# Running sums carried to all partitions by a DRAM scratch and repeating loads, where a selecting matmul did it: a two-layer hybrid block on one NeuronCore

## The chip, the core and the metric

One core of a Trainium2 chip (trn2) runs the whole program in one launch. The metric is the device time of an execution in microseconds (us); lower is better. The kernel before takes 1228.23 us (median of three runs).

## What is computed

The reference passes 256 tokens of width 1024 through two layers. A layer is a gated feed-forward, a mixer and a second feed-forward, each added to the residual. The mixer projects the normed input to 6232 columns: a state-space branch (z, a short convolution, step sizes dt) and an attention branch (q, k, v and an index that picks 64 keys per query). The change touches the state-space branch alone. With one chunk of 256 tokens it comes down to this:

```python
def ssd_chunked(xh, dt, a, bmat, cmat, chunk):
    x = xh * dt[..., None]
    adt = dt * a                                  # 256 tokens x 16 heads
    a_cs = jnp.cumsum(adt, axis=-1)               # the running sums
    seg = a_cs[..., :, None] - a_cs[..., None, :]
    decay = exp(where(tril, seg, -inf))           # 256 x 256 for each head
    cb = einsum('bclgn,bcsgn->bcgls', cc, bc)
    y_diag = einsum('bcgls,bcgels,bcsgep->bclgep', cb, decay, x)
    ...
```

For each of 16 heads the matrix of decays needs the running sum of the column's token (one number a partition, which an engine takes as a per-partition bias) and that of the row's token: a row of 256 numbers that must stand in all 128 partitions. How that row gets to all partitions is what changes.

## The kernel before

All weights stream through three raw buffers of 1 MB (`Stream`): SyncE issues the loads (L113), ScalarE rounds a block to `whi` (L126), VectorE takes the rest as `wlo` (L127), and TensorE multiplies three times, high by high, high by low, low by high (`three`, L181 to L183; the convolution's columns at L887 to L889). Three split blocks exist at a time, so a block is split when TensorE has used up the one three before it.

The mixer (`mixer`) walks `MIX_ORDER`: index columns, z and convolution columns, then q, k and v in units of 512 columns, two token tiles each. A unit's bank is drained by one ScalarE instruction (L915 for q and k, L912 for v), GpSimd rotates q and k (`rope`, L406 to L409), and TensorE transposes them (`turn`, L866). Between these units generators are stepped that hold the side work: `steps` (dt and the running sums), `index` (scores at L655 and L660, then the top 64), `ssd` and `attention`. A scheduler sets the final order of each engine's instructions when the program is built; the engines then run their own lists in order and wait on semaphores.

The steps touched:

- `steps` makes the running sums `cs` (128 tokens x 2 tiles x 16 heads) with three small matmuls. It then splits them into a high and a low part, puts both into `c2` (16 high columns, a gap, 16 low columns), transposes `c2` in two matmuls (L626), and ScalarE copies the result to `csT` (64 x 256, L627).
- `ssd` goes over 2 groups of 8 heads in fours (`h0` of 0 and 4). For each four it takes a tile `m` from `six()` (two buffers, shared with the index's `idx_tm` and `idxT` and later with the attention); `m0` is 4 x 256, `m1` 4 x 128. Per head one matmul (L734) has a column of `pick`, repeated to 128 columns, as its stationary operand and `csT` as its moving one: it adds high and low part of one head's row and puts the row in all partitions of a PSUM bank of pool `sd`. ScalarE reads it twice (L740, L742: Relu of the difference from the per-partition sum), then takes two Exps for the four (L744, L745). VectorE multiplies with `dt` and the masked `cb` (L748, L750).
- After both fours TensorE forms y (L760, L764: 24 matmuls a group into two banks of `ac`); y of the first four can run before the second four is there. GpSimd (L774), VectorE (L780, L781, L788) and ScalarE (L438) finish y, and it is transposed for the output projection (L795).

Of the kernel before, what the change touches and what calls it, by code (L numbers as in the profile page):

```python
# [8 lines left out]
F32 = mybir.dt.float32  # L9
FR = mybir.dt.float32r  # L10
I32 = mybir.dt.int32
AF = mybir.ActivationFunctionType
ALU = mybir.AluOpType
AX = mybir.AxisListType

P = 128
# [36 lines left out]
def hybrid_kernel(  # L53
# [18 lines left out]
    tp = ctx.enter_context(tc.tile_pool(name="tp", bufs=2, space=PSUM))  # L72


    def bank(pool):
        return pool.tile([P, 512], F32, name=pool.name, tag=pool.name)
# [223 lines left out]
    pick_f = const.tile([64, H_SSD], F32, name="pick_f")  # L300
    nc.gpsimd.memset(pick_f, 0.0)
    for base in (0, 32):
        nc.gpsimd.affine_select(out=pick_f, in_=pick_f, compare_op=ALU.not_equal, fill=1.0,
                                base=-base, pattern=[[-1, H_SSD]], channel_multiplier=1)
    pick = const.tile([64, H_SSD], FR, name="pick")
    c2s = []
    for l in range(DEPTH):
        c2 = const.tile([P, NT, 64], F32, name=f"c2_{l}")
        nc.gpsimd.memset(c2, 0.0)
        c2s.append(c2)  # L310
# [24 lines left out]
    def setup():  # L335
# [4 lines left out]
        with tc.tile_pool(name="setup", bufs=1, reuse_waits="tile") as tmp:  # L340
# [15 lines left out]
            nc.vector.tensor_copy(pick, pick_f)  # L356
# [194 lines left out]
    def mixer(l, norm, after):  # L551
        with ExitStack() as mctx:
# [23 lines left out]
            csT = ms.tile([64, L], FR, name="csT")  # L576
# [6 lines left out]
            def steps():  # L583
# [34 lines left out]
                chi = ms.tile([P, NT, H_SSD], FR, name="chi")  # L618
                nc.vector.tensor_copy(chi, cs)
                c2 = c2s[l]  # L620
                nc.vector.tensor_copy(c2[:, :, 0:16], chi.bitcast(F32))
                nc.vector.tensor_sub(c2[:, :, 32:48], cs, chi.bitcast(F32))
                yield
                ps = bank(tp)
                for t in range(NT):
                    nc.tensor.transpose(ps[0:64, t * P:(t + 1) * P], c2[:, t], ident)  # L626
                nc.scalar.copy(csT, ps[0:64, :L])  # L627
# [85 lines left out]
            def ssd():  # L713
# [9 lines left out]
                for g in range(G_SSD):  # L723
                    ms4 = []
                    for h0 in (0, 4):
# [4 lines left out]
                        for h in (0, 2):  # L730
                            ps = bank(sd)
                            for j in range(2):
                                hh = 8 * g + h0 + h + j
                                nc.tensor.matmul(ps[:, j * L:(j + 1) * L],  # L734
                                                 pick[:, hh:hh + 1].to_broadcast([64, P]), csT,
                                                 start=True, stop=True)
# [270 lines left out]
```

## Time and profile before

| | |
|---|---|
| median of three runs | 1228.23 us (1227.38 to 1228.77) |
| the profiled execution's own time | 1228.15 us |
| its span in the trace | 1226.4 us |
| granted TensorE clock, mean | 0.998 |
| TensorE busy | 99% of the span |
| VectorE, ScalarE, GpSimd busy | 60%, 51%, 8% |

The span runs from the first to the last instruction; 1.75 us of the execution lie around it. Layer 0's mixer has its running sums and decays between 255 and 355 us, layer 1's 603 us later.

### The profile page before, as it was taken

The numbers are of one execution on the slowest core, as the hardware profiler recorded it, in microseconds if no ns is written. First come the engines' busy times: TensorE is split into PE (matmuls) and PEld (weight loads), VectorE is DVE, ScalarE is ACT, GpSimd is POOL, SyncE is SP. The second block draws the span as 40 slices with busy tenths as digits, with TensorE's granted clock in tenths as the row PEclk, the third lists the DMA queues.
The fourth block names the chain that finished last, engine by engine and source line by source line (L and its number), as shares of the span: only waits on it lengthen the run. The fifth ranks groups of instructions, "written<-read, shape, count | busy, mean of one in ns | idle before, by whom it ended". The sixth has DMA issues, their size and how long they took to land.

```text
span 1226.4 us, 15386 instructions
## 1 busy us (share of the span) xinstructions
PE 1211.1 (99%) x6031; PEld 1010.0 (82%) x6031; DVE 734.3 (60%) x970; ACT 629.8 (51%) x860; POOL 102.5 (8%) x209
## 2 busy tenths in 40 slices
PE   8999999999999999999999999999999999999997
PEld 6788889988888888888888888898977888888886
DVE  5655545785687565554465554476858866555543
ACT  5544435656676454444354444366567655444432
POOL 0200000601220000000000000024112100000000
PEclk9999999999999999999999999999999999999999
DMA  8665555654233555655646645465442445556550
GB/s 256 195 206 174 187 177 167 213 170 167 99 138 110 166 184 167 199 197 181 201 151 196 197 168 201 158 214 175 155 154 84 157 155 161 179 175 206 179 198 35
DMA packets 147820, 210.02 MB, mean 171 GB/s; under 512 B 7908, under 2 KB 115108, under 8 KB 147748
## 3 DMA queue, kind: packets, MB, share of 16 engines
q1 hardware_dynamic: 147604, 208.52, 51.5%
q8 instruction: 47, 0.77, 0.3%
q10 hardware_dynamic: 144, 0.52, 0.1%
q14 instruction: 25, 0.20, 0.0%
HBM read 207.98 MB, written 1.05 MB: 170 GB/s over the span
## 4 chain that ended last, share of the span: by engine, by line
PE 93%; DVE 3%; DMA 1%; ACT 1%; POOL 1%; issue 0%; SPq 0%; POOLq 0%; ACTq 0%; DVEq 0%
PE mm L181 15%; PE mm L182 15%; PE mm L183 15%; PE ac L183 12%; PE ac L181 12%; PE ac L182 12%; PE tp L522 2%; PE ac L760 1%; PE mm L887 1%; PE mm L889 1%; PE ac L889 1%; PE mm L888 1%; PE ac L887 1%; PE ac L888 1%; DVE wlo L127 1%; PE sd L655 1%
## 5 line engine op out<-in xcount | busy, mean ns | idle before, releaser
L127 DVE TENSOR_TENSOR wlo<-raw,whi 128x2048 fp32r<-128x2048 f32 (+3 forms) x206 | 451.2, 2195 | 337.3 <-ACT whi L126 336.9
L126 ACT CAST whi<-raw 128x2048 fp32r<-128x2048 f32 (+3 forms) x206 | 377.0, 1836 | 304.4 <-PE ac L183 187.1
L181 PE MATMUL mm<-whi,tT 128*128 128x512 f32 (+1 forms) x672 | 268.4, 399 | 0.0
L182 PE MATMUL mm<-wlo,tT 128*128 128x512 f32 (+1 forms) x672 | 260.8, 388 | 2.8 <-DVE wlo L127 2.8
L183 PE MATMUL mm<-whi,tT 128*128 128x512 f32 (+1 forms) x672 | 261.7, 389 | 0.4 <-DVE tT L418 0.4
L181 PE MATMUL ac<-whi,tT 128*128 128x512 f32 (+1 forms) x480 | 190.4, 397 | 0.9 <-ACT whi L126 0.5
L182 PE MATMUL ac<-wlo,tT 128*128 128x512 f32 (+1 forms) x480 | 184.8, 385 | 0.8 <-DVE wlo L127 0.8
L183 PE MATMUL ac<-whi,tT 128*128 128x512 f32 (+1 forms) x480 | 185.4, 386 | 0.0
L182 PEld LDWEIGHTS mm<-wlo,tT 128*128 128x128 f32 x672 | 126.5, 188 | 27.1 <-DVE wlo L127 3.5
L183 PEld LDWEIGHTS mm<-whi,tT 128*128 128x128 f32 x672 | 126.2, 188 | 27.2 <-issue 1.3
L181 PEld LDWEIGHTS mm<-whi,tT 128*128 128x128 f32 x672 | 126.4, 188 | 23.4 <-ACT s L912 0.7
L182 PEld LDWEIGHTS ac<-wlo,tT 128*128 128x128 f32 x480 | 90.4, 188 | 17.7 <-DVE wlo L127 1.8
L181 PEld LDWEIGHTS ac<-whi,tT 128*128 128x128 f32 x480 | 90.2, 188 | 17.8 <-ACT whi L126 1.2
L183 PEld LDWEIGHTS ac<-whi,tT 128*128 128x128 f32 x480 | 90.2, 188 | 17.7
L432 POOL TENSOR_TENSOR r_x<-ms_x,mhalf 128x1 f32<-128x1 f32 x14 | 9.7, 695 | 873.6 <-DVE ms_x L430 866.1
L181 PE MATMUL ac<-whi,hT_hi 128*128 128x512 f32 x176 | 69.3, 394 | 0.0
L181 PE MATMUL mm<-whi,hT_hi 128*128 128x512 f32 x176 | 69.0, 392 | 0.0
L183 PE MATMUL ac<-whi,hT_lo 128*128 128x512 f32 x176 | 68.6, 390 | 0.0
L183 PE MATMUL mm<-whi,hT_lo 128*128 128x512 f32 x176 | 68.6, 390 | 0.0
L182 PE MATMUL mm<-wlo,hT_hi 128*128 128x512 f32 x176 | 68.5, 389 | 0.0
L182 PE MATMUL ac<-wlo,hT_hi 128*128 128x512 f32 x176 | 68.5, 389 | 0.0
L544 ACT ACTIVATE s1k<-ac,r_x 128x256 f32<-128x256 f32 x44 | 20.6, 471 | 67.6 <-PE ac L183 64.7
(222 smaller groups left out, 1463.7 us busy)
## 6 DMA issues: line engine op xcount, KB each, us to landing
raw<-in_w_ffn_in_dram SPq DMA_DIRECT2D x172, 512.0 KB, 4.9
raw<-in_w_ffn_out_dram SPq DMA_DIRECT2D x44, 1024.0 KB, 4.8
raw<-in_w_mix_in_dram SPq DMA_DIRECT2D x44, 1024.0 KB, 5.2
raw<-in_w_mix_out_dram SPq DMA_DIRECT2D x16, 1024.0 KB, 4.8
raw<-in_w_mix_in_dram SPq DMA_DIRECT2D x4, 600.0 KB, 3.8
raw<-in_w_mix_in_dram SPq DMA_DIRECT2D x4, 568.0 KB, 3.8
raw<-in_w_ffn_in_dram SPq DMA_DIRECT2D x8, 256.0 KB, 3.5
h_res<-in_x_dram SPq DMA_DIRECT2D x4, 256.0 KB, 3.6
```

The costliest lines, as they stand in the source:

```text
L126: pin(nc.scalar.copy(hi[:, o], raw[:, o]))
L127: pin(nc.vector.tensor_sub(lo[:, o], raw[:, o], hi[:, o].bitcast(F32)))
L181: nc.tensor.matmul(ps, xh, whi, start=first, stop=False)
L182: nc.tensor.matmul(ps, xh, wlo, start=False, stop=False)
L183: nc.tensor.matmul(ps, xl, whi, start=False, stop=last)
L522: nc.tensor.transpose(ps[:, f * L + t * P:f * L + (t + 1) * P], hs[:, t, f * P:(f + 1) * P], ident)
L544: nc.scalar.activation(sg, ps[:, 0:256], AF.Silu, scale=norm.r[t])
L655: nc.tensor.matmul(pse[j % 2][:, j // 2 * nk:(j // 2 + 1) * nk], idxT[b0:b0 + 64, h // 2, t * P:(t + 1) * P], idxT[b0:b0 + 64, 4, 0:nk], s ...
L760: nc.tensor.matmul(o, m0[:, h % 4, t * P:(t + 1) * P], half[:, 0, h * 64:(h + 1) * 64], start=True, stop=(t == 0))
L887: nc.tensor.matmul(ps, hi[:, o:o + P], xh, start=(k == 0), stop=False)
L888: nc.tensor.matmul(ps, hi[:, o:o + P], xl, start=False, stop=False)
L889: nc.tensor.matmul(ps, lo[:, o:o + P], xh, start=False, stop=(k == KD - 1))
```

## The change

The row of a head no longer comes from a matmul. `csT` is now the plain transpose of `cs` (32 x 128, one matmul, no split into high and low). GpSimd's queue writes it to a scratch tile in DRAM, `csum` (16 heads x 256 tokens, two DMAs of 8 KB). For each four heads one DMA on the same queue then reads four rows of `csum` (4 KB) once for each partition into `m0`: 512 KB a load, four loads a layer. ScalarE computes `m1` and then `m0` in place from what was loaded. `pick`, `c2` and their set-up go.

```diff
--- before.py
+++ after.py
@@ -70,6 +70,7 @@
     ac = ctx.enter_context(tc.tile_pool(name="ac", bufs=2, space=PSUM))
     sd = ctx.enter_context(tc.tile_pool(name="sd", bufs=2, space=PSUM))
     tp = ctx.enter_context(tc.tile_pool(name="tp", bufs=2, space=PSUM))
+    rowsums = ctx.enter_context(tc.tile_pool(name="rowsums", bufs=2, space=bass.MemoryType.DRAM))
 
 
     def bank(pool):
@@ -297,17 +298,6 @@
     nc.gpsimd.memset(causneg, 0.0)
     nc.gpsimd.affine_select(out=causneg[:, P:], in_=causneg[:, P:], compare_op=ALU.is_ge, fill=NEG,
                             base=0, pattern=[[-1, P]], channel_multiplier=1)
-    pick_f = const.tile([64, H_SSD], F32, name="pick_f")
-    nc.gpsimd.memset(pick_f, 0.0)
-    for base in (0, 32):
-        nc.gpsimd.affine_select(out=pick_f, in_=pick_f, compare_op=ALU.not_equal, fill=1.0,
-                                base=-base, pattern=[[-1, H_SSD]], channel_multiplier=1)
-    pick = const.tile([64, H_SSD], FR, name="pick")
-    c2s = []
-    for l in range(DEPTH):
-        c2 = const.tile([P, NT, 64], F32, name=f"c2_{l}")
-        nc.gpsimd.memset(c2, 0.0)
-        c2s.append(c2)
     gains = const.tile([P, 64], F32, name="gains")
     convs = const.tile([P, 120], F32, name="convs")
     heads = const.tile([P, 3, DEPTH, H_SSD], F32, name="heads")
@@ -353,7 +343,6 @@
             yield
             for i, v in enumerate((dt_bias, a_log, d_skip)):
                 later(heads[:, i], v.partition_broadcast(P))
-            nc.vector.tensor_copy(pick, pick_f)
             yield
             pg = bank(tp)
             nc.tensor.transpose(pg[:, 0:64], rows, ident[:64, :64])
@@ -573,7 +562,8 @@
             rb = ms.tile([P, L], F32, name="rb")
             dt = ms.tile([P, NT, H_SSD], F32, name="dt")
             cs = ms.tile([P, NT, H_SSD], F32, name="cs")
-            csT = ms.tile([64, L], FR, name="csT")
+            csT = ms.tile([NT * H_SSD, P], F32, name="csT")
+            csum = rowsums.tile([H_SSD, L], F32, name="csum", tag="csum")
             sz, xs = (big8().rearrange("p (t c) -> p t c", t=NT) for _ in range(2))
             kT, qT = (big8().rearrange("p (h c) -> p h c", h=H_ATT) for _ in range(2))
             vv = big8().rearrange("p (t c) -> p t c", t=NT)
@@ -615,16 +605,12 @@
                 nc.tensor.matmul(ps[:, 16:32], ones, adt[:, 0], start=True, stop=False)
                 nc.tensor.matmul(ps[:, 16:32], triu, adt[:, 1], start=False, stop=True)
                 nc.vector.tensor_copy(cs.rearrange("p t h -> p (t h)"), ps[:, 0:32])
-                chi = ms.tile([P, NT, H_SSD], FR, name="chi")
-                nc.vector.tensor_copy(chi, cs)
-                c2 = c2s[l]
-                nc.vector.tensor_copy(c2[:, :, 0:16], chi.bitcast(F32))
-                nc.vector.tensor_sub(c2[:, :, 32:48], cs, chi.bitcast(F32))
                 yield
                 ps = bank(tp)
+                nc.tensor.transpose(ps[0:NT * H_SSD, 0:P], cs.rearrange("p t h -> p (t h)"), ident)
+                nc.scalar.copy(csT, ps[0:NT * H_SSD, 0:P])
                 for t in range(NT):
-                    nc.tensor.transpose(ps[0:64, t * P:(t + 1) * P], c2[:, t], ident)
-                nc.scalar.copy(csT, ps[0:64, :L])
+                    nc.gpsimd.dma_start(csum[:, t * P:(t + 1) * P], csT[t * H_SSD:(t + 1) * H_SSD, :])
                 yield
 
 
@@ -727,20 +713,13 @@
                         m0 = m[:, 0:1024].rearrange("p (h c) -> p h c", h=4)
                         m1 = m[:, 1024:1536].rearrange("p (h c) -> p h c", h=4)
                         ms4.append((m0, m1))
-                        for h in (0, 2):
-                            ps = bank(sd)
-                            for j in range(2):
-                                hh = 8 * g + h0 + h + j
-                                nc.tensor.matmul(ps[:, j * L:(j + 1) * L],
-                                                 pick[:, hh:hh + 1].to_broadcast([64, P]), csT,
-                                                 start=True, stop=True)
-                            for j in range(2):
-                                hh = 8 * g + h0 + h + j
-                                row = ps[:, j * L:(j + 1) * L]
-                                nc.scalar.activation(m0[:, h + j], row, AF.Relu, scale=-1.0,
-                                                     bias=cs[:, 0, hh:hh + 1])
-                                nc.scalar.activation(m1[:, h + j], row[:, P:], AF.Relu, scale=-1.0,
-                                                     bias=cs[:, 1, hh:hh + 1])
+                        hh = 8 * g + h0
+                        nc.gpsimd.dma_start(m0, csum[hh:hh + 4, :].partition_broadcast(P))
+                        for h in range(4):
+                            nc.scalar.activation(m1[:, h], m0[:, h, P:], AF.Relu, scale=-1.0,
+                                                 bias=cs[:, 1, hh + h:hh + h + 1])
+                            nc.scalar.activation(m0[:, h], m0[:, h], AF.Relu, scale=-1.0,
+                                                 bias=cs[:, 0, hh + h:hh + h + 1])
                         nc.scalar.activation(m0, m0, AF.Exp, scale=-1.0)
                         nc.scalar.activation(m1, m1, AF.Exp, scale=-1.0)
                         for h in range(4):
```


The order of the lists moves as well. Line numbers of the changed kernel differ: there L181 to L183 are L182 to L184, L655 is L641, L660 is L646, L740 and L742 are L721 and L719, L744 and L745 are L723 and L724, L760 and L764 are L739 and L743, L774 is L753, L866 is L845 and L915 is L894. `s6` is a tile of `six()`, `s2` one of a rotated or scored block, `s8_1650` the state-space input by token, `mm` and `ac` PSUM banks.

GpSimd's list in layer 0, from the transposed sums on, in the changed kernel:

```order
L398 TENSOR_TENSOR s2_2460<-s1k_2462,s1k_2463 128x4x32 [waits Pool_49]
L613 DMA csum_1648<-csT_1647 16x128 [waits Activation_49]
L613 DMA csum_1648<-csT_1647 16x128
L717 DMA s6_2703<-csum_1648 128x1024 [waits DMASW1_49,DMASW0_49,PE_49]
L395 TENSOR_TENSOR s1k_2519<-s2_2517,cc_att_121 128x128 [waits Activation_49]
L396 TENSOR_TENSOR s1k_2520<-s2_2517,ss_att_122 128x4x16 [waits Pool_49]
```

The two writes and the first load stand between two rotations of q; nothing of this is in the list before. `DMASW` is the landing of a DMA from this queue.

GpSimd's list around the second load, before:

```order
L406 TENSOR_TENSOR s1k_2835<-s2_2833,cc_att_132 128x128 [waits Activation_49]
L407 TENSOR_TENSOR s1k_2836<-s2_2833,ss_att_133 128x4x16
L408 TENSOR_TENSOR s1k_2836<-s2_2833,ss_att_133 128x4x16
L409 TENSOR_TENSOR s2_2833<-s1k_2835,s1k_2836 128x4x32 [waits DVE_49,PE_49,Pool_49]
L774 TENSOR_TENSOR s8_1661<-s8_1661,heads_130 128x512 [waits DMAHW5_49,PE_49]
L774 TENSOR_TENSOR s8_1661<-s8_1661,heads_130 128x512 [waits PE_49]
```

and in the changed kernel:

```order
L398 TENSOR_TENSOR s2_2809<-s1k_2811,s1k_2812 128x4x32 [waits DVE_49,PE_49,Pool_49]
L717 DMA s6_2789<-csum_1648 128x1024 [waits DMAHW3_49,DMAHW2_49,DMAHW4_49,DMAHW1_49,DMAHW7_49,DMAHW0_49,PE_49]
L717 DMA s6_2959<-csum_1648 128x1024 [waits PE_49]
L395 TENSOR_TENSOR s1k_2904<-s2_2902,cc_att_121 128x128 [waits Activation_49]
L396 TENSOR_TENSOR s1k_2905<-s2_2902,ss_att_122 128x4x16
L397 TENSOR_TENSOR s1k_2905<-s2_2902,ss_att_122 128x4x16
L398 TENSOR_TENSOR s2_2902<-s1k_2904,s1k_2905 128x4x32 [waits DVE_49,Pool_49]
L753 TENSOR_TENSOR s8_1650<-s8_1650,heads_119 128x512 [waits DMAHW5_49,PE_49]
L753 TENSOR_TENSOR s8_1650<-s8_1650,heads_119 128x512 [waits PE_49]
L717 DMA s6_3046<-csum_1648 128x1024 [waits DVE_49]
```

Second and third load follow each other, ahead of a rotation and of the work on y; the second waits for TensorE's last score matmul (its buffer is that of `idxT`), the third for y of the first four heads. The DMAHW waits are for loads of the first 60 us.

ScalarE's list at the second four heads of group 0, before:

```order
L126 CAST whi_2888<-raw_2711 128x2048 [waits DMAHW3_49,PE_49]
L867 COPY s8_1663<-tp_2892 128x4x128 [waits PE_49]
L740 ACTIVATE s6_2808<-sd_2809,cs_1658 128x256 [waits PE_49]
L742 ACTIVATE s6_2808<-sd_2809,cs_1658 128x128
L740 ACTIVATE s6_2808<-sd_2809,cs_1658 128x256
L742 ACTIVATE s6_2808<-sd_2809,cs_1658 128x128
```

and in the changed kernel:

```order
L127 CAST whi_2864<-raw_2697 128x2048 [waits DMAHW3_49,PE_49]
L719 ACTIVATE s6_2789<-s6_2789,cs_1646 128x128 [waits DMASW3_49]
L719 ACTIVATE s6_2789<-s6_2789,cs_1646 128x128
L721 ACTIVATE s6_2789<-s6_2789,cs_1646 128x256 [waits Activation_49] x2
L719 ACTIVATE s6_2789<-s6_2789,cs_1646 128x128 x2
L721 ACTIVATE s6_2789<-s6_2789,cs_1646 128x256 [waits Activation_49] x2
L724 ACT_TABLE_LOAD
L724 ACTIVATE s6_2789<-s6_2789 128x512
L723 ACTIVATE s6_2789<-s6_2789 128x1024 [waits Activation_49]
L646 ACTIVATE s2_2846<-sd_2837 128x512 [waits PE_49,Pool_49]
L846 COPY s8_1652<-tp_2868 128x4x128
L894 ACTIVATE s2_2902<-mm_2817,r_x_1698 128x512 [waits DVE_49]
```

The Relus now wait for a landing in place of a matmul, one more table load stands ahead of the Exps, and a bank's drain (L894) stays behind them.

TensorE's list at y of the second four heads, in the changed kernel:

```order
L845 MATMUL tp_2943<-ident_99,s2_2809 128x128 [waits PE_49,Pool_49]
L845 MATMUL tp_2943<-ident_99,s2_2809 128x128 x3
L739 MATMUL ac_2874<-s8_1650,s6_2789 128x64 [waits DVE_49]
L739 MATMUL ac_2875<-s8_1650,s6_2789 128x64
L743 MATMUL ac_2875<-s8_1650,s6_2789 128x64
L739 MATMUL ac_2874<-s8_1650,s6_2789 128x64 [waits DVE_49]
L739 MATMUL ac_2875<-s8_1650,s6_2789 128x64
L743 MATMUL ac_2875<-s8_1650,s6_2789 128x64
L739 MATMUL ac_2874<-s8_1650,s6_2789 128x64 [waits DVE_49]
L739 MATMUL ac_2875<-s8_1650,s6_2789 128x64
L743 MATMUL ac_2875<-s8_1650,s6_2789 128x64
L182 MATMUL mm_2987<-whi_2699,tT_1506 128x512 [waits Activation_49]
```

These matmuls stand after 24 matmuls of the unit k1 (`mm_2910`); before, they stood among the second half of the same 24. The score matmuls (L641), which stood among these too, are moved ahead of y of the first four, in groups of four where they stood in pairs.

## Rows read from the trace of the kernel before

**Rows 1.** The page, part 1: busy time of the engines.
```profile
PE 1211.1 (99%) x6031; PEld 1010.0 (82%) x6031; DVE 734.3 (60%) x970; ACT 629.8 (51%) x860; POOL 102.5 (8%) x209
```

**Rows 2.** The page, part 4: the chain that ended last, by engine.
```profile
PE 93%; DVE 3%; DMA 1%; ACT 1%; POOL 1%; issue 0%; SPq 0%; POOLq 0%; ACTq 0%; DVEq 0%
```

**Rows 3.** What TensorE waited for: us in total, times, longest.
```profile
PE mm L182 <- DVE wlo L127: 2.8, 2, 1.4
```

**Rows 4.** The selecting matmuls of both layers, by source line.
```profile
L734 PE MATMUL sd<-csT,pick x32: 272/279/382, 300.1 to 941.7; 64*128 64x256 f32 x32
```

**Rows 5.** TensorE's timeline, layer 0: start, us, engine, line, count.
```profile
299.56 0.39 PE L182 MATMUL mm<-wlo,tT 128*128 128x512 f32 x1
299.78 0.39 PE L183 MATMUL mm<-whi,tT 128*128 128x512 f32 x1
300.10 0.73 PE L734 MATMUL sd<-csT,pick 64*128 64x256 f32 x4
300.76 0.50 PE L181 MATMUL mm<-whi,tT 128*128 128x512 f32 x1
301.10 0.40 PE L182 MATMUL mm<-wlo,tT 128*128 128x512 f32 x1
...
303.93 1.13 PE L655 MATMUL sd<-s 64*128 64x256 f32 x4
...
309.85 0.50 PE L734 MATMUL sd<-csT,pick 64*128 64x256 f32 x2
310.28 0.66 PE L866 MATMUL tp<-ident,s 128*128 128x128 f32 x4
...
311.46 0.39 PE L181 MATMUL mm<-whi,tT 128*128 128x512 f32 x1
...
312.20 0.50 PE L182 MATMUL mm<-wlo,tT 128*128 128x512 f32 x1
```

**Rows 6.** DMA issues: KB each, us from issue to landing.
```profile
fin<-in_final_norm_dram ACTq DMA_DIRECT2D x1, 512.0 KB, 3.8
...
out_dram<-h_res SPq DMA_DIRECT2D x4, 128.0 KB, 1.9
...
heads<-in_d_skip_dram SPq DMA_DIRECT2D x1, 16.0 KB, 6.0
```

**Rows 7.** Windows around the fin load and in layer 0's mixer.
```profile
1005.00:1012.00 7.00, 7.00 (x34) 5.90 (x33) 1.85 (x6) 2.70 (x4) 0.00 (x0) 1.00 0.67 225
275.00:345.00 70.00, 68.59 (x368) 55.91 (x367) 46.89 (x88) 47.93 (x81) 16.67 (x33) 1.00 0.35 120
```

**Rows 8.** ScalarE's timeline: csT, and the first four heads.
```profile
276.79 0.37 ACT L627 CAST csT<-tp 64x256 fp32r<-64x256 f32 x1
...
302.07 0.46 ACT L740 ACTIVATE s<-sd,cs 128x256 f32<-128x256 f32 x1
...
304.67 1.28 ACT L744 ACT_TABLE_LOAD   x1
...
307.45 0.67 ACT L915 ACTIVATE s<-mm,r_x 128x512 f32<-128x512 f32 x1
```

**Rows 9.** ScalarE and TensorE before the second four heads.
```profile
317.07 1.90 ACT L126 CAST whi<-raw 128x2048 fp32r<-128x2048 f32 x1 [0.81 <-PE mm L183]
...
317.31 1.23 PE L760 MATMUL ac<-s,s 128*128 128x64 f32 x10
...
319.91 0.48 PE L181 MATMUL mm<-whi,tT 128*128 128x512 f32 x1
```

**Rows 10.** VectorE's line that scales the masked decays.
```profile
L748 DVE SCALAR_TENSOR_TENSOR s<-s,dt,cb x32: 470/483/750, 307.1 to 953.4; 128x256 f32<-128x256 f32 x32
```

**Rows 11.** GpSimd beside a low-part split, and later alone.
```profile
283.31 2.29 DVE L127 TENSOR_TENSOR wlo<-raw,whi 128x2048 fp32r<-128x2048 f32 x1 [0.42 <-ACT whi L126]
...
283.94 1.98 POOL L406 TENSOR_TENSOR s1k<-s,cc_att 128x128 f32<-128x128 f32 x1 [6.96 <-ACT s L915]
...
294.20 0.46 POOL L406 TENSOR_TENSOR s1k<-s,cc_att 128x128 f32<-128x128 f32 x1 [7.18 <-ACT s L915]
```


## The prediction

> **What bounds the kernel now.** I read the page first: TensorE is busy for 99% of the span [rows 1], and the chain of work that ended last runs through it for 93% [rows 2]. The reader is to see that this kernel is a TensorE queue: an instruction taken out of that queue shortens the end by its length, and work on another engine costs nothing until TensorE waits for it. The second view is therefore TensorE's waits. In the mixers there is one kind worth naming, two waits of 1.4 us, one in each layer, for a low part of the weights (`wlo`) that VectorE makes late [rows 3]. The third is TensorE's own timeline in the mixer, because a busy share doesn't tell what a matmul costs: the recorded durations overlap (0.39 us each, while the starts are 0.22 apart [rows 5]), so I price by differences of starts.
>
> **What goes from TensorE.** The selecting matmuls are 32 records, 16 in a layer, in both mixers [rows 4]. The first four start at 300.10; the main matmul ahead of them started at 299.78 and would have been followed 0.23 later. The two main matmuls behind start at 300.76 and 301.10. Without the four the second would have started at 299.78 + 2 x 0.23 = 300.24, so the four cost 0.86 us: 0.66 for themselves, and 0.09 and 0.11 for leaving and re-entering the main stream. Two more stand in groups of four, which I price alike. The second four heads of group 0 come in pairs: one between transposes takes 0.43 (309.85 to 310.28), one alone 0.74 between two main starts (311.46 to 312.20), which is 0.51 more than 0.23, and with 0.11 behind it 0.62 [rows 5]. A layer: 3 x 0.86 + 0.43 + 0.62 = 3.63 us; two layers 7.3 us.
>
> One of two transposes of the sums goes too, about 0.1 us in a layer by the four transposes of 0.41 us from 310.28 on (four records, 0.66 long, overlapping) [rows 5]: 0.2 us. The three small VectorE copies of the high and low part go from an engine that is 60% busy [rows 1], and I count nothing for them.
>
> The order gives a little more. The scores (L655) of the last index tile stand in four pairs between main matmuls, and in two groups of four after the change. A pair is recorded with 1.13 us; it costs 0.20 more for leaving and re-entering the stream, as above. Two interruptions fewer are 0.4 us a layer, 0.8 us in all. Together TensorE loses 7.3 + 0.2 + 0.8 = 8.3 us of work.
>
> **What is added, and its price.** GpSimd's queue issues no DMA in this trace, so its price has to be bounded. Nearest in shape is `fin`: one 4 KB row repeated to 128 partitions, 512 KB, issued by ScalarE's queue, 3.8 us from issue to landing [rows 6]. It landed while the DMA engines were 67% busy at 225 GB/s; the mixer runs at 35% and 120 GB/s [rows 7], so neither the repeated row nor the weight stream should make our loads slower than that. The other end is the slowest of the small repeated loads, `heads` with 6.0 us, which queued behind others [rows 6]. As the issuing engine is a different one, I take 5 us, between the two, and keep 3.8 to 6.0. For the write of `csum` the store of 128 KB gives 1.9 us and `heads` again 6.0 [rows 6]; I take 2.5, near the store.
>
> By the Trainium skill (DMA: Bandwidth & Descriptors, section on the anatomy of one DMA on the gpsimd path) such a DMA takes a fixed 2.0 us and its bytes at 436 GB/s, an estimate of 3.2 us for 512 KB; with it the charge below for late loads would go, and the time would be 1219.9 us. The row of `fin` says 3.8, and my sum goes by rows.
>
> **Does a load hold up TensorE?** Four loads a layer, in turn.
>
> First load: `csT` is ready at 277.2 [rows 8], the write lands near 279.7, the load near 284.7. ScalarE then has Relus (2.6 us for eight), one table load of 1.28 and Exps (together 2.78 to the next instruction [rows 8]), and in the changed list also a second table load, a `whi` of 1.9 [rows 9] and some six rows of about half a microsecond before it drains the bank of q1's first tile: about 12 us. TensorE wants that bank when q1 ends, near 299.9, where the first selecting matmul stood [rows 5]. So the load may land up to 287.8, 8.1 us after its issue. It does no harm. Behind it on GpSimd stands a rotation of q that can't start before 283.9 anyway [rows 11].
>
> Second load: this is the tight one. It waits for the last score matmul, since its buffer is that of `idxT`. Y of the first four starts at 317.31 now [rows 9]. Ahead of it 1.9 us of selecting matmuls go, and two score pairs (2 x 1.1) move in: about 317.6. The last score stands 12 main matmuls (2.7 us) and a turn (0.3) ahead of that: the load is issued at 314.5. Y of the first four takes 2.6 us (317.31 to 319.91 [rows 9]), 24 main matmuls 5.5, a turn 0.3: TensorE wants y of the second four at 326.2. From the landing on it takes Relus 2.6, table load and Exps 2.78 [rows 8], one scaling 0.48 on VectorE [rows 10]: 5.9 us. So the load must have landed by 320.3, and may take 5.8 us. ScalarE itself isn't free before 319.1, as it first rounds a block that TensorE releases near 317.2 [rows 9]. With 5 us the margin is 0.8; with 6.0 the wait is 0.2. Since four heads are scaled one after another I charge 0.5 us a layer, 1.0 us in all. Queued behind the Relus on ScalarE are the drain of the unit k0 and the next `whi`; both are wanted about 2 us after y.
>
> Third and fourth load are issued when y of the first four, and GpSimd's work on group 0, are done; ScalarE comes to them 6 and 8 us later by the same count, so they are hidden. If loads took 8 us, only the third would add its own wait.
>
> The added table loads (two a layer, 1.28 us each [rows 8]) lie on ScalarE, 51% busy [rows 1]; in the spans above they are counted. The weights' loads lose bandwidth to 4.2 MB more, against a mixer at 35% of the DMA engines [rows 7]: nothing. Should that cover go, TensorE would wait for raw blocks, which it does nowhere now.
>
> **Sum.** Against the profiled execution's own 1228.15 us (the median is 1228.23, 0.08 above): - 7.3 - 0.2 - 0.8 + 1.0 = - 7.3, so 1220.9, which I round to **1221 us**. The two `wlo` waits I leave as they are. From here on, 0.2% (about 2.5 us) is what a measurement of this kernel tells from no change.
>
> **Rivals.**
>
> *Better:* no charge for the second load, and the `wlo` waits go as well, since ScalarE's list around them moves. For it: the fin row's 3.8. Against: these waits depend on VectorE's list, which I can't time. 1228.15 - 8.3 - 2.8 = 1217.0; this case holds 1217 to 1219.5.
>
> *GpSimd can't write the DMA's descriptions while VectorE holds it off.* A rotation step takes 1.98 us beside a `wlo` of 2.29, and 0.46 alone [rows 11]. If an issue is held the same way, and the second load's issue falls at the start of a `wlo`, it lands 2.2 us later: 7.2 us, 1.4 over the allowed 5.8, so 1.4 a layer in place of 0.5: 1222.7, up to 1225.5 when the third is held too. This is the one rule that speaks against the change: the Trainium skill (SBUF — State Buffer, section SBUF: two separate sides) says that a DMA issued from GpSimd starves while VectorE runs an operation that takes both port pairs, and advises another queue. By the Trainium skill, on the same page, a two-input operation shuts out only GpSimd's reads; the row of 1.98 agrees that reads are held, and no run here shows an issue.
>
> *The gain is eaten:* loads of 8.4 to 9.6 us. Beyond 5.8 each microsecond at the second load, and beyond 8.1 also at the first, goes to TensorE's wait: at 9.0 us it is 3.2 + 0.9 = 4.1 a layer, the whole of 8.3. It gives 1225.7 to 1230.7.
>
> *Slower:* the same place, with loads above 9.6 us, two and a half times the fin row: 1231 and more; at 12 us 6.2 + 3.9 a layer, 1240. For it: an unpriced queue, a scratch written and read back in one go, and in-order lists on GpSimd and ScalarE that put rotations and bank drains behind the landing. Against: every transfer in the trace lands in 6.0 or less.
>
> That the change doesn't do what it says isn't a rival: the changed list shows no selecting matmul.
>
> **Chances.** Forecast, 1219.5 to 1222.5: 0.45. Better: 0.15. Held issue, 1222.5 to 1225.7: 0.14. Eaten: 0.12. Slower: 0.14. Faster by over 0.2% are the first three, 0.74; within 0.2% 0.12; slower 0.14. The range of 8 in 10 goes from 1217, the best sum, into the eaten case, 1229; above it lie the slower case and a part of the eaten one. The likeliest case's own range is 1219.5 to 1222.5.
>
> **What the profile after would show.** TensorE's busy time some 8 us less, with no `csT` matmul. Loads `s6 <- csum`, 512 KB, near 5 us from issue to landing; writes of `csum` near 2.5. A wait of TensorE (or of its weight loads) for VectorE's scaling at y of the second four below 1 us a layer. ScalarE waiting for the first landing about 1 us, without TensorE waiting in turn. The forecast falls if the second load takes over 6 us, if GpSimd is busy for microseconds per issue, or if TensorE waits for a bank that ScalarE drains late.

## The result, and the profile after

The changed kernel takes 1215.09 us (median of 4 runs, 1214.89 to 1215.76) beside 1227.89 us of the kernel before on the same chip: the ratio is 0.9895, with an interval from 0.9883 to 0.9908. It is faster by 12.8 us. 1221 us was forecast, with a range that began at 1217. The direction and the first mechanism were right; the gain is 5.5 us larger than the sum's 7.3.

The page of the kernel after, part 1, part 4 (the chain that ended last) and the loads of part 6. The answering rows of before are [rows 1] and [rows 2]:

```profile
PE 1198.1 (99%) x5997; PEld 1003.0 (83%) x5997; DVE 729.4 (60%) x963; ACT 636.6 (52%) x864; POOL 112.8 (9%) x216
...
PE 93%; DVE 2%; ACT 2%; DMA 1%; POOL 1%; issue 0%; SPq 0%; ACTq 0%; POOLq 0%; DVEq 0%
...
s<-csum POOLq DMA_DIRECT2D x8, 512.0 KB, 4.0
```

The span went from 1226.4 to 1213.5 us, by 12.9, and TensorE's busy time from 1211.1 to 1198.1, by 13.0. So the time came out of TensorE's own list. 34 of its records are gone: the 32 of [rows 4] and two transposes. The forecast took 8.3 us of work from TensorE; 13.0 went. The next view shows where the rest was. TensorE's timeline of the kernel after, at the first score group of the second index tile (L641, which was L655):

```profile
302.37 0.39 PE L184 MATMUL mm<-whi,tT 128*128 128x512 f32 x1
302.69 1.14 PE L641 MATMUL sd<-s 64*128 64x256 f32 x8
303.76 0.50 PE L182 MATMUL mm<-whi,tT 128*128 128x512 f32 x1
304.09 0.40 PE L183 MATMUL mm<-wlo,tT 128*128 128x512 f32 x1
```

The eight records are four matmuls, and they take 1.14 us. Before, a pair (four records) took 1.13 us at 303.93 [rows 5]. Four now cost what two cost. In starts: 302.37 to 303.76 is 1.39, less the 0.23 of a main matmul 1.16, and 0.10 more behind it: 1.26 us for a group. TensorE's timeline of the kernel before, around that pair and the next:

```profile
303.61 0.39 PE L181 MATMUL mm<-whi,tT 128*128 128x512 f32 x1
...
304.99 0.50 PE L182 MATMUL mm<-wlo,tT 128*128 128x512 f32 x1
305.42 1.13 PE L655 MATMUL sd<-s 64*128 64x256 f32 x4
306.48 0.50 PE L183 MATMUL mm<-whi,tT 128*128 128x512 f32 x1
306.81 0.39 PE L181 MATMUL mm<-whi,tT 128*128 128x512 f32 x1
```

From 303.61 to 306.81 are 3.20 us for two pairs and three main matmuls; less 3 x 0.23 a pair cost 1.25 us. Four pairs a layer became two groups, 2.5 us a layer and 5.0 in all, where the forecast has 0.8.

What TensorE waited for, kernel after (total, times, longest):

```profile
PE tp L845 <- ACT s L696: 1.6, 2, 0.8
...
PE tp L774 <- DVE s L767: 0.7, 2, 0.3
...
PE mm L182 <- ACT s L894: 0.5, 2, 0.2
```

The two waits of 1.4 us for `wlo` in the mixers [rows 3] are not in this answer any more. In their place stand 0.8 us a layer at transposes of q (their PSUM bank is drained late by ScalarE's L696), and two smaller ones. A wait for a bank that ScalarE drains late was one of the signs by which the prediction said it would fall; here it costs 1.6 us in all and decides nothing. There is no wait at y of the second four heads, on which the forecast put 1.0 us: the second load was issued at 313.25 and landed in 4.0 us, and ScalarE came to it without a wait. Layer 0 on GpSimd, ScalarE and TensorE:

```profile
313.25 0.61 POOL L717 DMA_DIRECT2D s<-csum  x1 [3.34 <-PE sd L641]
...
317.69 0.69 ACT L719 ACTIVATE s<-s,cs 128x128 f32<-128x128 f32 x2
...
324.30 0.60 PE L845 MATMUL tp<-ident,s 128*128 128x128 f32 x4
324.73 0.56 PE L739 MATMUL ac<-s,s 128*128 128x64 f32 x4
```

### The profile page after: what moved, and what is told of

Same layout as the page of the kernel before. It is cut to its first block, busy times and chain, and to the rows that moved or that the text cites. A ratio compares the mean times of both kernels' runs of the same rounds, so it can differ in the third digit from the quotient of the medians.

```text
span 1213.5 us, 15334 instructions
## 1 busy us (share of the span) xinstructions
PE 1198.1 (99%) x5997; PEld 1003.0 (83%) x5997; DVE 729.4 (60%) x963; ACT 636.6 (52%) x864; POOL 112.8 (9%) x216
## 4 chain that ended last, share of the span: by engine, by line
PE 93%; DVE 2%; ACT 2%; DMA 1%; POOL 1%; issue 0%; SPq 0%; ACTq 0%; POOLq 0%; DVEq 0%
PE mm L182 15%; PE mm L184 15%; PE mm L183 15%; PE ac L183 12%; PE ac L184 12%; PE ac L182 12%; PE tp L511 2%; PE ac L739 1%; DMA raw<-in_w_ffn_in_dram 1%; PE mm L866 1%; PE ac L868 1%; PE mm L868 1%; PE ac L867 1%; PE mm L867 1%; PE ac L866 1%; PE sd L800 1%
## 5 line engine op out<-in xcount | busy, mean ns | idle before, releaser
L182 PE MATMUL mm<-whi,tT 128*128 128x512 f32 (+1 forms) x672 | 267.6, 398 | 0.5 <-ACT s L894 0.5
L184 PE MATMUL mm<-whi,tT 128*128 128x512 f32 (+1 forms) x672 | 260.8, 388 | 0.4 <-DVE tT L407 0.4
L183 PE MATMUL mm<-wlo,tT 128*128 128x512 f32 (+1 forms) x672 | 260.1, 387 | 0.0
L182 PE MATMUL ac<-whi,tT 128*128 128x512 f32 (+1 forms) x480 | 190.0, 396 | 1.0 <-ACT tT L405 0.5
L183 PE MATMUL ac<-wlo,tT 128*128 128x512 f32 (+1 forms) x480 | 185.1, 386 | 0.8 <-DVE wlo L128 0.8
L184 PE MATMUL ac<-whi,tT 128*128 128x512 f32 (+1 forms) x480 | 185.2, 386 | 0.0
L184 PEld LDWEIGHTS mm<-whi,tT 128*128 128x128 f32 x672 | 126.2, 188 | 26.0 <-DVE tT L407 0.9
L182 PEld LDWEIGHTS mm<-whi,tT 128*128 128x128 f32 x672 | 126.3, 188 | 25.1 <-issue 1.3
L183 PEld LDWEIGHTS mm<-wlo,tT 128*128 128x128 f32 x672 | 126.5, 188 | 22.7 <-DVE wlo L128 0.2
L182 PEld LDWEIGHTS ac<-whi,tT 128*128 128x128 f32 x480 | 90.2, 188 | 17.9 <-ACT whi L127 1.2
L183 PEld LDWEIGHTS ac<-wlo,tT 128*128 128x128 f32 x480 | 90.4, 188 | 17.6 <-DVE wlo L128 1.9
L184 PEld LDWEIGHTS ac<-whi,tT 128*128 128x128 f32 x480 | 90.2, 188 | 17.7
L182 PE MATMUL ac<-whi,hT_hi 128*128 128x512 f32 x176 | 69.2, 393 | 0.0
L182 PE MATMUL mm<-whi,hT_hi 128*128 128x512 f32 x176 | 69.0, 392 | 0.0
L184 PE MATMUL ac<-whi,hT_lo 128*128 128x512 f32 x176 | 68.6, 390 | 0.0
L184 PE MATMUL mm<-whi,hT_lo 128*128 128x512 f32 x176 | 68.6, 390 | 0.0
L183 PE MATMUL mm<-wlo,hT_hi 128*128 128x512 f32 x176 | 68.5, 389 | 0.0
L183 PE MATMUL ac<-wlo,hT_hi 128*128 128x512 f32 x176 | 68.5, 389 | 0.0
```

Of the source, the lines that this page charges most:

```text
L182: nc.tensor.matmul(ps, xh, whi, start=first, stop=False)
L183: nc.tensor.matmul(ps, xh, wlo, start=False, stop=False)
L184: nc.tensor.matmul(ps, xl, whi, start=False, stop=last)
```

## The experiments

Three theories stood after the traces. **A**: matmuls on the two 64-row halves of TensorE run at the same time when they stand side by side, so the regrouped scores brought about 5 us. **B**: regrouping saves only the interruptions, 0.8 us as forecast, and the rest comes from waits. **C**: the selecting matmuls cost more than the 7.3 us that the forecast gave them.

**Order within a group.**

```diff
-for j in range(2 * per):
+for j in (0, 2, 1, 3) if t else range(2 * per):
```

> The changed kernel; of each four score matmuls of the second tile the two on the lower 64 rows stand first, then the two on the upper ones. Theory A (matmuls on different 64-row halves run side by side): four in turn cost 1.26 us of TensorE's queue, two of one half already 1.25, so a second pair adds 1.06 to each group; 2 groups in 2 layers give + 4.2 us on 1215.1: 1219.3 us. Theory B (a group costs the same in any order, and the gain beyond the forecast came from vanished waits): 1215.1, within 0.5.

Measured: 1214.72 us, ratio 0.9894 (0.9880 to 0.9907), the same as the changed kernel's. The expectation of A was wrong in this form; the number is that of B, whose reason (waits that vanished) the next run refuses. TensorE's list now names both matmuls of the lower rows and then both of the upper ones, with every other row as it was, and the group on TensorE's timeline takes:

```profile
301.68 1.14 PE L641 MATMUL sd<-s 64*128 64x256 f32 x8
```

So the order inside the group doesn't matter. This leaves two readings: halves overlap whatever the order, or a group has one price, whatever it holds. The next run changes the grouping alone.

**Grouping alone, in the kernel before.** The first matmul of a group gets one more dependency, on the last reader of the other bank, so that both banks are free when it starts.

```diff
+if t and j == 0:
+    tc.add_manual_dep(ins.ins, reader[-1].ins.name, mybir.DependencyInfo(
+        mybir.DependencyClass.Sync, mybir.DependencyReason.DATA),
+        reason="both banks")
```

> The kernel before, its selecting matmuls kept; the first score matmul of a group of the second tile also waits for the other bank's reader, so that the four stand together and change halves in turn, as in the changed kernel. Theory A (halves side by side): four pairs of 1.25 us become two groups of 1.26, - 2.5 us a layer, - 5.0 in all: 1222.9 us. Theory B (only the interruptions count, as forecast): - 0.8 us: 1227.1. The waits for the low part of the weights stay in either.

Measured: 1223.47 us, ratio 0.9964 (0.9952 to 0.9977): 4.4 us faster than before, between 2.8 and 5.9. A's 5.0 lies in it, B's 0.8 doesn't. No load, no scratch and no selecting matmul was changed; on TensorE's list the scores moved, and with them some main matmuls and matmuls of y beside them. TensorE's timeline of this kernel:

```profile
304.44 1.14 PE L655 MATMUL sd<-s 64*128 64x256 f32 x8
```

And what TensorE waited for:

```profile
PE mm L182 <- DVE wlo L127: 2.8, 2, 1.4
```

TensorE is busy for 1206.1 us here, 5.0 less than before. About 0.6 us of the shorter span lie ahead of the mixers, where nothing was changed (the first score group starts at 252.2 us and not at 252.8); the rest is the 4.4 of the runs. The waits for `wlo` are still there in full, so the 4.4 us owe nothing to them. That a group has one price whatever it holds is against the pair of before: two matmuls of one half alone take 1.13 us, so two more of the same half could not be free. The row that shows the overlap had been in the trace of before all along; the prediction didn't read it. It is the first index tile's group on TensorE's timeline, eight matmuls of 128 columns, four on each half:

```profile
252.83 1.16 PE L655 MATMUL sd<-s 64*128 64x128 f32 x16
```

That is 1024 columns in 1.16 us, while a pair of one half [rows 5] needs 1.13 us for 512. The Trainium skill (TensorEngine Tiling (Array Packing), section Theoretical Speedup) states a factor of up to two for a contraction of at most 64 rows, with two tiles at once; this row and the groups of four agree with it.

**The selecting matmuls put back.** The changed kernel with 16 matmuls a layer of the same shape, into banks that nobody reads. Their operands are zeros, so they add work that serves nothing.

```diff
 nc.gpsimd.dma_start(m0, csum[hh:hh + 4, :].partition_broadcast(P))
+for h in (0, 2):
+    ps = bank(sd)
+    for j in range(2):
+        c = hh + h + j
+        nc.tensor.matmul(ps[:, j * L:(j + 1) * L],
+                         pick[:, c:c + 1].to_broadcast([64, P]), rows_fr,
+                         start=True, stop=True)
```

> The changed kernel with sixteen selecting matmuls a layer put back, into banks that nobody reads, at the places in the program where they stood, on constant operands; loads and Relus stay as changed. Theory A (the forecast's price holds): + 7.3 us on 1215.1: 1222.4 us, 1221.5 to 1223.5 with the waits they may move. Theory B (the whole 12.8 us are theirs, by bank or stream effects): 1227 or more.

Measured: 1223.40 us, ratio 0.9963 (0.9950 to 0.9975), 8.3 us above the changed kernel; each of the two ratios is uncertain by 1.5 us. The 7.3 of the forecast lies within that; C, which wanted all 12.8, doesn't. On its timeline a group costs 0.86 us once more (0.97 between two main starts, less 0.23, and 0.12 behind):

```profile
302.23 0.39 PE L184 MATMUL mm<-whi,tT 128*128 128x512 f32 x1
302.54 0.73 PE L728 MATMUL sd<-rows_fr,pick 64*128 64x256 f32 x4
303.20 0.51 PE L182 MATMUL mm<-whi,tT 128*128 128x512 f32 x1
303.55 0.40 PE L183 MATMUL mm<-wlo,tT 128*128 128x512 f32 x1
```

The two runs add up: 4.4 for the grouping and 8.3 for the selecting matmuls are 12.7, beside 12.8 for the change. With 1.5 us of uncertainty on each, the agreement is closer than the runs can show.

**How much room the second load has.** The same lists on all engines, but the scratch's rows lie in pieces of 512 bytes.

```diff
-csum = rowsums.tile([H_SSD, L], F32, name="csum", tag="csum")
+csum = rowsums.tile([H_SSD, L // 128, 256], F32, name="csum", tag="csum")
...
-nc.gpsimd.dma_start(m0, csum[hh:hh + 4, :].partition_broadcast(P))
+nc.gpsimd.dma_start(m0.rearrange('p h (k c) -> p h k c', c=128),
+                    csum[hh:hh + 4, :, 0:128].partition_broadcast(P))
```

> The changed kernel, every engine's list the same; the scratch holds its rows in pieces of 512 bytes with gaps, so a load is 1024 pieces in place of 128 and lands later. ScalarE comes to the second load 4.4 us after its issue. Theory A (no slack behind that, as the count of the forecast has it): each microsecond of landing above 4.4 us shows as a wait of TensorE at y of the second four heads, so a landing of 6.5 us costs 2.1 a layer: 1219.3 us. Theory B (hidden with room): 1215.1, within 0.5, with the same landing.

Measured: 1215.30 us, ratio 0.9896 (0.9881 to 0.9911), no change. The second load landed 1.1 us later, and ScalarE waited for it; TensorE's start of y moved from 0.43 to 0.54 us behind the transposes ahead of it. The second load of layer 0 among the DMA issues:

```profile
s<-csum POOLq DMA_DIRECT2D x1, 512.0 KB, 5.1
```

ScalarE and TensorE in the timeline:

```profile
318.50 0.70 ACT L719 ACTIVATE s<-s,cs 128x128 f32<-128x128 f32 x2 [0.61 <-DMA s<-csum]
...
324.40 0.60 PE L845 MATMUL tp<-ident,s 128*128 128x128 f32 x4
324.94 0.66 PE L739 MATMUL ac<-s,s 128*128 128x64 f32 x4
```

A delay of 0.7 us at ScalarE reached TensorE as 0.1. So behind the 4.4 us at which ScalarE arrives there is about 0.6 us of room: a load may take 5.0 us, where the forecast's count allowed 5.8, and theory A of this run was too strict by the 0.6.

**Pieces of 256 bytes.** The same edit with 64 in place of 128. The program's lists differ in places.

> The changed kernel; the scratch holds its rows in pieces of 256 bytes with gaps, 2048 pieces a load, where 1024 of 512 bytes landed 5.1 us after the issue at the second load and cost TensorE 0.1. ScalarE's, VectorE's and TensorE's lists differ in places from the changed kernel's. Theory A (room for 0.6 us behind 4.4, each further microsecond is TensorE's wait at y of the second four): a landing of 7 us costs 2.0 a layer: 1219 us. Theory B (hidden with room): 1215.1, within 1.

Measured: 1218.95 us, ratio 0.9925 (0.9912 to 0.9937). The number is that of A, the reason isn't: the second load landed in 7.2 us, but TensorE's waits are others, since the lists had moved.

```profile
PE tp L845 <- ACT s L696: 3.2, 2, 1.7
PE mm L183 <- DVE wlo L128: 2.5, 2, 1.3
```

ScalarE waited 8.1 us in all for landings, and what stood behind on its list came late. This run doesn't size the room at y.

**The pairs apart, in the changed kernel.** The upper half's matmuls wait until ScalarE has read the lower half's bank.

```diff
+if t and j == 1:
+    tc.add_manual_dep(ins.ins, rd.ins.name, mybir.DependencyInfo(
+        mybir.DependencyClass.Sync, mybir.DependencyReason.DATA), reason="apart")
```

> The changed kernel; of the four score matmuls of a group of the second tile the two on the upper 64 rows wait until ScalarE has read the two on the lower rows, so main matmuls stand between them, as in the kernel before. Theory A (two halves run at once when their matmuls stand together in the list, in whatever order; apart, each pair costs 1.25 us): + 2.5 us a layer on 1215.1: 1220.1 us, 1219 to 1222 with the waits it may move. Theory B (standing together is worth only the interruption, 0.2 us each): 1215.9.

Measured: 1233.29 us, ratio 1.0037 (1.0023 to 1.0051): 0.0142 above the changed kernel's ratio, 17.4 us. Both expectations were far too low. The pairs are back at 1.13 us each, which is the 5.0:

```profile
302.66 1.13 PE L642 MATMUL sd<-s 64*128 64x256 f32 x4
...
304.84 1.13 PE L642 MATMUL sd<-s 64*128 64x256 f32 x4
```

The rest began there: the last score comes later, the second load (which waits for it) is issued at 316.81 and not at 313.25, 0.15 us behind a weight load, and lands in 6.6 us. The first window is that of the load, the others stretch from TensorE's wait on (columns: length, busy times, granted clock, DMA share, GB/s):

```profile
316.80:323.40 6.60, 6.60 (x45) 5.92 (x44) 4.40 (x8) 2.87 (x3) 1.15 (x2) 1.00 0.82 275
...
327.00:330.00 3.00, 0.09 (x1) 0.09 (x1) 1.68 (x6) 2.99 (x5) 0.11 (x1) 0.83 0.31 118
330.00:333.00 3.00, 3.00 (x14) 2.90 (x14) 2.56 (x7) 3.00 (x10) 1.94 (x4) 0.50 0.00 0
333.00:336.00 3.00, 3.00 (x14) 2.96 (x14) 0.00 (x0) 1.52 (x3) 0.62 (x1) 0.50 0.00 0
336.00:339.00 3.00, 3.00 (x8) 2.31 (x7) 2.24 (x4) 0.17 (x1) 1.96 (x3) 0.50 0.08 31
339.00:342.00 3.00, 3.00 (x14) 2.46 (x13) 3.00 (x8) 3.00 (x6) 1.71 (x4) 0.96 0.37 143
...
936.00:946.00 10.00, 10.00 (x43) 8.85 (x42) 6.58 (x16) 6.46 (x17) 5.08 (x9) 0.66 0.18 54
```

TensorE in the timeline of layer 0:

```profile
329.91 1.11 PE L742 MATMUL ac<-s,s 128*128 128x64 f32 x4 [3.25 <-DVE s L730]
```

TensorE waits 3.25 us at y of the second four heads in layer 0, and from there its granted clock is 0.50 (1.2 GHz, the lower of its two levels) until past 339. Half of the 9.3 us from 329.91 to about 339.2 is 4.6 us. In layer 1 the wait is 3.0 (of 6.2 for both), and 10 us at a mean of 0.66 lose 3.4. The sum is 5.0 for pairs, 6.2 for waits and 8.0 for the clock, less the 2.8 of waits that the changed kernel has and this one hasn't: 16.4, where the spans, 1230.4 and 1213.5, are 16.9 apart.

**The loads alone, in the kernel before.** Transpose, scratch and loads are added, the selecting matmuls stay, and the Relus overwrite what the loads brought.

```diff
...
+nc.gpsimd.dma_start(m0, csum[c:c + 4, :].partition_broadcast(P))
 for h in (0, 2):
     ps = bank(sd)
```

> The kernel before, selecting matmuls kept, with the changed kernel's transpose, scratch writes and four loads a layer added; each load fills the tile that the Relus then overwrite from PSUM. Theory A (the loads cost TensorE nothing, the forecast's 1.0 us for the second one was wrong): only the added transpose, 0.2 us in all: 1228.1 us, within 1. Theory B (the loads do cost, and the other terms of the change are larger still): 1229.5 or more.

Measured: 1244.98 us, ratio 1.0140 (1.0126 to 1.0154), 16.7 us slower. The number lies in B's open range, but neither theory had the way it came about. In this kernel the tile of the second four heads comes free only when y of the first four is done, so its load is issued at 319.95 and lands in 6.8 us; ScalarE waits, and the two score banks, filled by selecting matmuls, wait for ScalarE's Relus. TensorE's last scores wait for the banks. The load among the DMA issues:

```profile
s<-csum POOLq DMA_DIRECT2D x1, 512.0 KB, 6.8
```

ScalarE and TensorE in the timeline:

```profile
327.10 0.47 ACT L750 ACTIVATE s<-sd,cs 128x256 f32<-128x256 f32 x1 [8.09 <-DMA s<-csum]
...
328.50 2.07 PE L663 MATMUL sd<-s 64*128 64x256 f32 x4 [3.76 <-ACT s L752]
```

Two windows behind the wait:

```profile
330.00:333.00 3.00, 3.00 (x7) 1.66 (x6) 2.33 (x7) 1.64 (x3) 0.00 (x0) 0.50 0.00 0
333.00:336.00 3.00, 3.00 (x13) 2.23 (x12) 1.27 (x4) 1.72 (x4) 0.89 (x2) 0.50 0.22 57
```

So this run doesn't price the loads in the changed kernel, where no Relu holds a score bank. It shows what the same loads cost where something waits for them: 3.76 us, and the clock behind it.

**A fourth buffer, and halves.** Three runs looked for a faster version by taking the changed kernel's waits away. The first gives ScalarE's query units a fourth buffer.

```diff
-s2 = mctx.enter_context(tc.tile_pool(name=f"s2_{l}", bufs=3, reuse_waits="tile"))
+s2 = mctx.enter_context(tc.tile_pool(name=f"s2_{l}", bufs=4, reuse_waits="tile"))
```

> The changed kernel with four buffers of 128 x 512 in place of three for query units and score rows (the tile s2). ScalarE then needn't wait 1.2 us for VectorE's score sums ahead of q's unit, and the drains behind it come earlier. Theory A (this is what TensorE waits for at the transposes of q, 0.8 us a layer): - 1.6 us on 1215.1: 1213.5 us. Theory B (the next thing behind it is as late): 1215.1, within 0.5.

Measured: 1217.12 us, ratio 0.9908 (0.9894 to 0.9921), no gain, and neither theory's number. The wait at L845 went as A has it, and the waits for `wlo` came back:

```profile
PE mm L183 <- DVE wlo L128: 3.1, 2, 1.5
```

Behind the first of the two, in layer 0, TensorE's granted clock was 0.50 for 3.4 us, which is 1.7 us more; behind the second, just as long, it stayed at 1.00. Windows of this kernel right behind each wait:

```profile
340.00:343.00 3.00, 3.00 (x9) 2.32 (x8) 2.93 (x6) 3.00 (x8) 0.84 (x3) 0.50 0.81 254
...
940.00:943.00 3.00, 3.00 (x26) 2.82 (x25) 2.93 (x10) 3.00 (x11) 1.59 (x4) 1.00 1.03 422
```

There are no selecting matmuls in this kernel. So the waits for `wlo` hang on how the lists of ScalarE and VectorE fall out, and that the change had removed them was no property of it. The next two split each weight block in two halves.

```diff
-parts = 2 if 3 <= self.split < 6 else 1
+parts = 2
```

> The changed kernel with every weight block rounded and split into its low part in two halves, not one piece. Theory A (TensorE wants only the first half when it comes to a block, and a wait for a low part, where the list makes one, is shorter): the changed kernel has one such wait of 0.8 us, so 1214.5 us, 1213.5 to 1215.5. Theory B (more and smaller instructions, 0.1 us each, delay ScalarE's and VectorE's other work): 1216 to 1218.

> The changed kernel with the fourth buffer of 128 x 512, which took the 1.6 us of waits at the transposes of q away and brought 3.1 us of waits for low parts, and with every weight block split in two halves. Theory A (the halves take the new waits away, and the gain of the buffer stays): 1213.5 us. Theory B (the waits move once more): 1216 to 1218.

Measured: the halves alone 1217.71 us, ratio 0.9922 (0.9905 to 0.9939), in the range of B, with waits at L774 of 1.5 us in each layer; halves and fourth buffer 1214.94 us, ratio 0.9888 (0.9875 to 0.9901), between its two theories, which can't be told from the changed kernel. Its mixers still show 0.6 to 0.7 us a layer at L774 and 0.3 to 0.4 for `wlo`. No version that is clearly better than the changed kernel was found.

## Why the prediction was right in its direction and wrong in its size

**The step that failed** is "Two interruptions fewer are 0.4 us a layer, 0.8 us in all". It took a pair's 1.13 us as the price of two matmuls wherever they stand, and so gave a group of four twice that. Side by side the two halves run at once, and the term is 4.4 us by the run of the kernel before with the scores grouped, 5.0 by starts on the timelines. With 5.0 in place of 0.8 the forecast's sum is 1216.7 us, and without its charge of 1.0 it is 1215.7. The list had shown the new grouping; the price was taken from a row in which only one half is at work.

**The selecting matmuls** were priced rightly by starts: 7.3 forecast, 8.3 measured as the difference of two ratios that are each uncertain by 1.5 us, and 0.86 us for a group of four in the trace of the kernel with them put back.

**The charge for the second load**, 1.0 us, was not there. A load took 4.0 us, near the row of `fin` [rows 6] and not 5, and ScalarE was the later one, as the forecast's count had it. Where that count allowed a load 5.8 us, the run with pieces of 512 bytes shows 5.0, so the place was tighter than forecast, and the load's 4.0 us stayed below that. The write of `csum` landed in 1.6 to 1.8 us, not 2.5.

**The `wlo` waits** were left as they are; 2.8 us of them went, and 2.8 came in other places (1.6, 0.7 and 0.5). That the rival *Better* names them was right in the profile and worth nothing in the sum. That leaving them out of the sum came out even is luck.

With these, for the profiled executions: - 7.3 - 0.2 - 5.0 - 2.8 + 2.8 = - 12.5, beside 12.9 in the spans.

**The weight stream** was said not to slow the loads. Some were slower beside it: the third load of layer 0, issued at 319.21, took 5.6 us with the DMA engines at 0.96, the first 4.0 at 0.46. Issue to landing of the two, kernel after:

```profile
s<-csum POOLq DMA_DIRECT2D x1, 512.0 KB, 4.0
...
s<-csum POOLq DMA_DIRECT2D x1, 512.0 KB, 5.6
```

And the windows of these two stretches:

```profile
280.30:284.30 4.00, 4.00 (x33) 3.87 (x32) 3.42 (x2) 2.62 (x3) 1.05 (x2) 1.00 0.46 150
...
319.20:324.80 5.60, 5.60 (x29) 4.60 (x28) 3.16 (x9) 5.57 (x10) 0.54 (x1) 1.00 0.96 319
```

It cost nothing there, as the third load is hidden, as forecast. The busy share alone doesn't give the length: in the kernel with the selecting matmuls put back a load took 4.1 us at 0.95 (its rows stand below). In these kernels the length goes with the weight load already under way at the issue: it landed 4.0 us behind the issue of the load of 5.6 us, 2.0 behind that of 4.6 us (the third of layer 1), 2.1 behind that of 4.1. But the load of 6.8 us in the kernel before had one that landed 3.8 us behind its issue, so what sets the length is not shown. In the run with the pairs apart the second load was issued 3.6 us later than in the changed kernel and took 2.6 us more; both together made it late.

The prediction's "every transfer in the trace lands in 6.0 or less" is misread: the list of DMA issues gives medians, and the weight loads of the kernel before take up to 8.0 us (median 4.9). So the argument against *Slower* was weaker than it stands there. The upper end of *The gain is eaten* comes to 1230.5 by its own prices, not 1230.7.

**The rival of the held issue** has no support. The third load was issued inside a low-part split of VectorE, but in the kernel with the selecting matmuls put back a load issued in the middle of such a split took 4.1 us, in the kernel before with the loads added one issued 0.3 us into a split of 2.29 us took 3.8, and the 6.6 us of the run with the pairs apart came with no split beside the issue. VectorE and GpSimd in the timeline of the kernel with the selecting matmuls put back:

```profile
923.07 2.29 DVE L128 TENSOR_TENSOR wlo<-raw,whi 128x2048 fp32r<-128x2048 f32 x1 [0.80 <-ACT whi L127]
...
924.47 0.53 POOL L723 DMA_DIRECT2D s<-csum  x1 [5.37 <-PE ac L756]
```

This load among the DMA issues:

```profile
s<-csum POOLq DMA_DIRECT2D x1, 512.0 KB, 4.1
```

An issue keeps GpSimd busy for 0.53 to 0.61 us in all eight loads of the changed kernel. By the Trainium skill (SBUF — State Buffer, section SBUF: two separate sides) it is operations that take both port pairs which starve such an issue; no run here shows an issue held in this way, and by this row the split with two inputs holds none.

**The slower rivals** had their place right, the second load, and their price too low: a wait of 3 us there was followed by the half clock in both slow kernels, which the prices of the eaten and the slower case left out.

What stays open is which row of the lists takes the `wlo` waits away, and whether the selecting matmuls put back cost more than 7.3 us. No wait hides in their 8.3: TensorE's waits in that kernel's mixers add up to 2.2 us, in the changed kernel's to 2.8. But they stand on its list as 4, 3, 1, 3, 1 and 4 a layer, before as 4, 2, 2, 4 and 4, and an interruption costs about 0.2 us by the forecast's own rows.

## What to carry to other kernels

Price a matmul that fills 64 rows from a row in which its neighbours are what they will be: beside a matmul on the other half it is nearly free, and alone it costs in full. A change that frees PSUM banks can regroup other matmuls, and this regrouping can be worth more than half of what the removed matmuls are; ask for it in the list, and look in the trace for a place where the new grouping already stands. A transfer that has 0.6 us of room is safe only as long as its issue doesn't slip into the next weight load.

## What the runs showed of the hardware

Matmuls of the two halves overlap even where the list names both of one half first (1.14 us for the four, in either order; the upper half's first record starts 0.014 us behind the lower half's first). The Trainium skill (TensorE: Matmul & The Clock Gate, section The mechanism) says that matmuls start and end in the list's order; four in 1.14 us with two of one half alone at 1.13 can't be had so, and here the measurement decides.

A repeated load of 512 KB through GpSimd's queue takes 3.7 to 4.0 us in the changed kernel with the DMA engines 37 to 46% busy, and 4.6 and 5.6 at 88 and 96%. In the two slow kernels the second load of a layer took 6.2 to 6.8 us at 82 to 100%: in one it was issued 0.15 us behind a weight load of 1 MB, in the other 1.8 us behind one, with the next issued 0.9 us later. The same load in pieces of 512 bytes takes 4.8 us in the median, in pieces of 256 bytes 5.9.

TensorE's waits of 2.9 to 3.8 us in the mixers of the two slow kernels were each followed by a stretch at a granted clock of 0.50. Those of 1.7 us and less in the other kernels' mixers left it at 1.00 (the kernel with pieces of 256 bytes has 1.5 and 1.3 in layer 0), but for one: a wait of 1.5 us in layer 0 of the kernel with the fourth buffer, with 3.4 us at 0.50 behind it.
